# Eleven orders of the 512 columns in the products of a macaron feed-forward

## The chip, the cores and the metric

The kernel runs on one core of a Trainium2 chip. The metric is the device time of one execution in microseconds (us). Before the change it is 1822.53 us, the median of two runs (1821.94 and 1823.11). The profiled execution took 1822.9 us; its span, from the first to the last instruction, is 1821.1 us.

## The reference

One decoder layer works on 256 tokens of width 2048, all in float32. What matters here is the two half-step feed-forwards, with 5632 hidden columns each:

```python
def swiglu_ffn(x, w_gate, w_up, w_down):
    return (jax.nn.silu(x @ w_gate) * (x @ w_up)) @ w_down

h = h + 0.5 * swiglu_ffn(rms_norm(h, ffn1_norm[l]), ffn1_w_gate[l], ffn1_w_up[l], ffn1_w_down[l])
...   # one input projection, windowed attention and a state-space branch, one output projection
h = h + 0.5 * swiglu_ffn(rms_norm(h, ffn2_norm[l]), ffn2_w_gate[l], ffn2_w_up[l], ffn2_w_down[l])
```

## The kernel before

**Products.** Every large product is a list of passes (class `Pass`). A pass makes 512 output columns for all 256 tokens, so it needs two accumulators of 128 rows by 512 columns, one PSUM bank each. The activations, transposed, are the stationary operand (128 by 128), and the weights are the moving operand (128 by 512). For more than one rounding's accuracy both are split into a high and a low part in a rounded float32 type. Each block of 128 weight rows then takes three matmuls for each half of the tokens: high by high, high by low, low by high.

**The passes of a feed-forward** are made in `ffn`: for each of 11 blocks of hidden columns (c from 0 to 10) a pass of gate and a pass of up, 16 row blocks each; then four passes of down (n from 0 to 3), 44 row blocks each. The layer runs the first feed-forward, then the mixer's passes, then the second feed-forward.

**One loop for all of them.** `run` walks through the passes in units of two row blocks. For each unit it issues the matmuls of line 363, which is where all these products show in the profile. The order of work is written out by hand: a weight tile of four row blocks (`raw`, three buffers) is loaded on SP's queue, ScalarE copies it into the rounded type (`wh`, line 318), VectorE subtracts to get the low part (`wl`, line 323), four buffers of each, two row blocks long. The side work (norms, attention, scan) is cut into steps that are taken between units.

**What reads the accumulators.** After the last matmul of a pass its `done` function reads both accumulators whole: SiLU on ScalarE for gate (line 394), a product on VectorE for up (line 405), the residual sum for down (lines 438 and 447).

**Where the operands lie.** The normalised activations are `xth` and `xtl` (high and low), the hidden ones lie in several tiles named `hid` in the profile. `gap` tiles of 8 floats stand between some of them, so that tiles start at other places modulo 64 bytes.

**Other matmuls**, on lines of their own, belong to the mixer and to transposes. Line 733 streams 128 adjacent columns of one tile; line 796 streams four runs of 32 columns, 512 elements apart; both load 32 stationary columns. Line 831 loads its 32 stationary columns 64 elements apart, and line 834 loads them adjacent. Line 525 transposes with stationary columns 16 elements apart.

Of the kernel before, what the change touches and what calls it, by code (L numbers as in the profile page):

```python
# [16 lines left out]
P = 128  # L17
# [18 lines left out]
WB = 4  # L36


class Pass:
    def __init__(self, w, n, stat, ks, done=None, delay=0, pre=None, box=None, opens=True, bank="acc", shared=False):  # L40
        self.w, self.n, self.stat, self.ks, self.done = w, n, stat, list(ks), done
        self.delay, self.pre, self.opens, self.bank = delay, pre, opens, bank
        self.box = {} if box is None else box
        self.shared = shared
# [3 lines left out]
def hybrid_layer_kernel(  # L48
# [8 lines left out]
    act, vec, pe, pool, sync = nc.scalar, nc.vector, nc.tensor, nc.gpsimd, nc.sync  # L57
# [13 lines left out]
    def nm(s):  # L71
        uid[0] += 1
        return f"{s}_{uid[0]}"
# [9 lines left out]
    def tps():  # L83
        return tpp.tile([P, 512], F32, name=nm("tp"), tag="tp")
# [53 lines left out]
    def split_plain(h, l, src):  # L138
        act.activation(out=h, in_=src, func=AF.Copy)  # L139
        vec.tensor_tensor(out=l, in0=src, in1=h.bitcast(F32), op=ALU.subtract)  # L140
# [3 lines left out]
    def by_blocks(src, dst, pause=3):  # L144
        turns[0] += 1
        b = const.tile([P, 4, NT, P], F32, name=nm("blocks"), tag="blocks")
        hd = h_d[turns[0] % 2]
        for t in range(NT):
            vec.transpose(out=b[:, :, t].rearrange("p j (k c) -> p j k c", k=4),  # L149
                          in_=src[:, t, :].rearrange("p (k j c) -> p j k c", k=4, j=4))  # L150
        yield
        sync.dma_start(out=hd.rearrange("j p x -> p j x"), in_=b.rearrange("p j t x -> p j (t x)"))
        yield 2
        for j in range(4):
            sync.dma_start(out=dst[32 * j:32 * j + 32].rearrange("r (i x) -> r i x", i=4),
                           in_=hd[j].rearrange("(i r) x -> r i x", i=4))
        yield pause
        return dst.rearrange("p (i t x) -> p i t x", i=4, t=NT)
# [79 lines left out]
    def spawn(g, delay=0):  # L238
        gens.append([g, delay])
        return g  # L240
# [7 lines left out]
    def step():  # L248
        for e in list(gens):
            if e[1] > 0:  # L250
                e[1] -= 1
            else:
                advance(e)

    def call(f, a):
        f(a)
        return
        yield

    def alive(g):  # L260
        return any(e[0] is g for e in gens)

    def finish(*gs):
        while any(alive(g) for g in gs):
            step()

    def run(passes, extra, start):
        groups = []
        passes = list(passes)
        while passes:  # L270
            p = passes.pop(0)
            if p.shared:
                q = passes.pop(0)
# [55 lines left out]
        def ahead(u):  # L329
            while st["dma"] < ng and st["dma"] < spent() + RAWB:  # L330
                dma()
            if st["split"] == 0:
                start()
            while st["split"] < 2 * ng and st["split"] <= (u + WB - 1 if u else 1):
                split()
                if st["split"] == 1:
                    start()
                while st["dma"] < ng and st["dma"] < spent() + RAWB:
                    dma()

        for u, (i, half) in enumerate(units):
            p, k0 = groups[i]
            if k0 == p.ks[0] and half == 0:
                if p.pre:
                    p.pre()
                if p.opens:
                    p.box["acc"] = [tps() if p.bank == "tp" else
                                    accp.tile([P, 512], F32, name=nm("acc"), tag="acc") for _ in range(NT)]
            acc = p.box["acc"]
            ahead(u)  # L350
            h, l = wts.pop(u)
            end = half == 1 and k0 == p.ks[-1]
            order = [(kk, t, v) for kk in range(2) for t in range(NT) for v in range(3)]
            if u == 0:
                order = [(kk, t, v) for v in (0, 2, 1) for kk in range(2) for t in range(NT)]
            elif end:
                order = [(kk, t, v) for t in range(NT) for kk in range(2) for v in range(3)]
            for kk, t, v in order:
                k = k0 + 2 * half + kk
                sh, sl = p.stat(k)  # L360
                first = p.opens and k == p.ks[0] and v == 0
                last = p.done is not None and k == p.ks[-1] + 3 and v == 2
                pe.matmul(acc[t], (sh, sh, sl)[v][:, t * P:(t + 1) * P], (h, l, h)[v][:, kk, :], start=first, stop=last)  # L363
            if end and p.done:
                spawn(call(p.done, acc), p.delay)
            step()


    def ffn(norm, w_gate, w_up, w_down, done, first):
        hid = {}  # L370
        sil = {}
        pairs = {}
        area = {}
        turn = {}

        def hidden(c):
            tag = HID[c]
            if tag in ("slot0", "slot3"):
                if tag not in pairs:
                    pairs[tag] = slots.tile([P, 2, 2, 4, SEQ], F32R, name=nm("hid"), tag=tag)  # L380
                    return pairs[tag][:, 0]
                return pairs[tag][:, 1]
            return slots.tile([P, 2, 4, SEQ], F32R, name=nm("hid"), tag=tag)

        def gate_done(c):
            def f(acc):
                def g():
                    while c >= 2 and alive(turn[c - 2]):
                        yield
                    if c == 0:  # L390
                        area["a"] = slots.tile([P, 2, NT, 512], F32, name=nm("sil"), tag="s5b")
                    sil[c] = area["a"][:, c % 2]
                    for t in range(NT):
                        act.activation(out=sil[c][:, t, :], in_=acc[t], func=AF.Silu, scale=norm.scale(t))  # L394
                for _ in g() if c < 2 or not alive(turn[c - 2]) else ():
                    pass
                if c not in sil:
                    spawn(g())
            return f

        def up_done(c):
            def f(acc):
                a = sil.pop(c)
                for t in range(NT):
                    vec.scalar_tensor_tensor(out=a[:, t, :], in0=acc[t], scalar=norm.scale(t),  # L405
                                             in1=a[:, t, :], op0=ALU.mult, op1=ALU.mult)

                def g():
                    yield
                    while (c >= 5 and first and alive(mx["pre"])) or (c and alive(turn[c - 1])):  # L410
                        yield
                    hid[c] = hidden(c)
                    turned = yield from by_blocks(a, a.rearrange("p t x -> p (t x)"), 6)
                    for t in range(NT):
                        h, l = (hid[c][:, v, :, t * P:t * P + P].rearrange("p k (i c) -> p k i c", c=32) for v in range(2))
                        split_plain(h, l, turned[:, :, t].rearrange("p i (k c) -> p k i c", k=4))

                turn[c] = spawn(g())
            return f

        def hstat(k):
            c, kk = divmod(k, 4)
            return hid[c][:, 0, kk, :], hid[c][:, 1, kk, :]

        ps = []
        for c in range(DFF // 512):
            ps.append(Pass(w_gate, c, norm.stat, range(0, KD, 4), gate_done(c), 2,
                           (lambda: finish(mx["pre"])) if c == 7 and first else None, shared=c == 0))
            ps.append(Pass(w_up, c, norm.stat, range(0, KD, 4), up_done(c), 2))
        for n in range(4):  # L430
            ps.append(Pass(w_down, n, hstat, range(0, DFF // P, 4), done(n), 2 if n < 3 else 0))
        return ps

    def residual(norm, factor):
# [687 lines left out]
    with tc.manual_schedule():  # L1122
# [14 lines left out]
        ps = tps()  # L1137
# [52 lines left out]
        def start():  # L1190
# [6 lines left out]
            mx["go"] = True  # L1197

        ff1 = ffn(n1, ffn1_w_gate[0], ffn1_w_up[0], ffn1_w_down[0], residual(nmix, 0.5), True)
        mixp = mixer(nmix, residual(n2, 1.0))  # L1200
        ff2 = ffn(n2, ffn2_w_gate[0], ffn2_w_up[0], ffn2_w_down[0], lambda n: final(n), False)

        def load_x(n):
# [8 lines left out]
        def extra(n):  # L1212
            load_x(n)
            if 0 <= n - at - 6 < 4:
                load_m1(n - at - 6)

        run(ff1 + mixp + ff2, extra, start)


# [52 lines left out]
```

## Time and profile before

| What | Value |
|---|---|
| median of the runs | 1822.53 us |
| profiled execution | 1822.9 us |
| its span | 1821.1 us |
| TensorE busy, instructions | 1814.7 us, 8383 |
| weight loads busy | 1470.7 us |
| VectorE busy | 1061.5 us |
| ScalarE busy | 845.3 us |
| DMA | 404.31 MB, mean 222 GB/s |

A busy time is the union of an engine's instructions, so overlapping matmuls count once. In the groups of instructions each line has the source line, engine, operation, output and inputs, shapes and count; then the busy time, the mean duration of one instruction in ns, and the idle time of the engine before them. Matmuls are pipelined: one starts before the last has ended, and the distance from start to start is read from counts in windows or from starts in the timeline. The chain of waits follows back from the last instruction to what released it.

### The profile page before, as it was taken

How to read it: one execution, taken by the hardware profiler on the slowest of the kernel's cores; microseconds unless marked ns; L12 is line 12 of the kernel's file. 1: busy time of each engine (PE TensorE's matmuls, PEld its weight loads, DVE VectorE, ACT ScalarE, POOL GpSimd, SP SyncE). 2: the span in 40 equal slices, each digit the busy share in tenths (PEclk: the TensorE clock that was granted, in tenths of full speed). 3: DMA queues.
4: the chain of work that ended last, by engine and by line, in shares of the span. 5: the costliest groups of instructions: out<-in, count | busy, mean ns of one | idle time of the engine just before them, and what ended most of it. 6: DMA issues, size and time to landing. Idle time of an engine off the chain costs nothing.

```text
span 1821.1 us, 21499 instructions
## 1 busy us (share of the span) xinstructions
PE 1814.7 (100%) x8383; PEld 1470.7 (81%) x8383; DVE 1061.5 (58%) x1380; ACT 845.3 (46%) x1087; POOL 80.3 (4%) x151
## 2 busy tenths in 40 slices
PE   9999999999999999999999999999999999999999
PEld 7788888888888888888888888888888888888887
DVE  5779897555555455554975665555555555544443
ACT  6454444444444444447766554444444444443332
POOL 0301222000000000010000001000000000000000
PEclk9999999999999999999999999999999999999999
DMA  7867888786665566698475576666666666665553
GB/s 273 239 222 238 288 277 282 227 235 209 212 221 204 195 213 223 216 327 262 161 263 197 203 249 201 217 215 209 208 208 211 211 216 214 216 203 209 205 196 104
DMA packets 213237, 404.31 MB, mean 222 GB/s; under 512 B 9756, under 2 KB 43125, under 8 KB 211472
## 3 DMA queue, kind: packets, MB, share of 16 engines
q1 hardware_dynamic: 204896, 380.66, 64.5%
q0 software_dynamic: 6416, 19.13, 3.5%
q10 hardware_dynamic: 1824, 3.15, 0.7%
q8 instruction: 65, 1.06, 0.2%
q14 instruction: 36, 0.29, 0.0%
HBM read 371.05 MB, written 34.48 MB: 223 GB/s over the span
## 4 chain that ended last, share of the span: by engine, by line
PE 96%; DVE 2%; ACT 1%; DMA 1%; issue 0%; SPq 0%; ACTq 0%
PE acc L363 92%; PE tp L363 1%; DMA raw<-in_ffn_w_gate_dram 1%; DVE wl L323 1%; DVE s1a L820 0%; ACT wh L318 0%; PE tp L831 0%; DVE s1a L821 0%; PE tp L796 0%; PE tp L733 0%; ACT tp L895 0%; PE tp L1006 0%; PE tp L834 0%; DVE slot L822 0%; PE tp L905 0%
## 5 line engine op out<-in xcount | busy, mean ns | idle before, releaser
L323 DVE TENSOR_TENSOR wl<-raw,wh 128x1024 fp32r<-128x1024 f32 x628 | 768.3, 1225 | 712.4 <-ACT wh L318 712.2
L318 ACT ACTIVATE wh<-raw 128x1024 fp32r<-128x1024 f32 (+1 forms) x636 | 672.1, 1058 | 909.0 <-PE acc L363 879.9
L363 PE MATMUL acc<-wh,xth 128*128 128x512 f32 x1664 | 661.5, 398 | 0.0
L363 PE MATMUL acc<-wl,xth 128*128 128x512 f32 x1664 | 659.3, 396 | 0.0
L363 PE MATMUL acc<-wh,xtl 128*128 128x512 f32 x1664 | 652.0, 392 | 0.2 <-DVE xtl L188 0.2
L363 PE MATMUL acc<-wh,hid 128*128 128x512 f32 x1408 | 437.7, 392 | 0.0
L363 PEld LDWEIGHTS acc<-wh,xth 128*128 128x128 f32 x1664 | 312.0, 188 | 77.6 <-issue 1.6
L363 PEld LDWEIGHTS acc<-wh,xtl 128*128 128x128 f32 x1664 | 312.5, 188 | 74.7 <-DVE xtl L188 0.6
L363 PEld LDWEIGHTS acc<-wl,xth 128*128 128x128 f32 x1664 | 312.9, 188 | 69.2 <-DVE wl L323 0.2
L363 PEld LDWEIGHTS acc<-wh,hid 128*128 128x128 f32 x1408 | 264.4, 188 | 58.9
L363 PE MATMUL acc<-wl,hid 128*128 128x512 f32 x704 | 276.2, 392 | 0.0
L363 PEld LDWEIGHTS acc<-wl,hid 128*128 128x128 f32 x704 | 132.3, 188 | 29.5
L133 POOL TENSOR_TENSOR rs_t<-rstds 128x2 f32<-128x2 f32 x9 | 3.6, 396 | 670.6 <-DVE rstds L125 670.1
L449 POOL DMA_DIRECT2D out_dram<-res x6 | 3.3, 550 | 648.6 <-DVE res L447 648.5
L405 DVE SCALAR_TENSOR_TENSOR sil<-acc,rstds,sil 128x512 f32<-128x512 f32 x44 | 30.8, 741 | 0.0
L149 DVE STREAM_TRANSPOSE blocks<-sil 128x512 f32<-128x512 f32 x44 | 28.5, 686 | 0.0
L140 DVE TENSOR_TENSOR hid<-sil,hid 128x512 fp32r<-128x512 f32 x44 | 28.3, 683 | 0.0
L394 ACT ACTIVATE sil<-acc,rstds 128x512 f32<-128x512 f32 x44 | 27.5, 677 | 0.0
L139 ACT ACTIVATE hid<-sil 128x512 fp32r<-128x512 f32 x44 | 25.0, 615 | 0.0
L363 PE MATMUL acc<-wh,s2a 128*128 128x512 f32 x64 | 21.1, 397 | 0.0
L363 PE MATMUL acc<-wh,s4b 128*128 128x512 f32 x64 | 20.9, 396 | 0.0
L363 PE MATMUL acc<-wh,slot 128*128 128x512 f32 x64 | 20.8, 394 | 0.0
(310 smaller groups left out, 780.0 us busy)
## 6 DMA issues: line engine op xcount, KB each, us to landing
raw<-in_ffn_w_down_dram SPq DMA_DIRECT2D x88, 1024.0 KB, 5.1
raw<-in_ffn_w_gate_dram SPq DMA_DIRECT2D x87, 1024.0 KB, 5.8
raw<-in_ffn_w_up_dram SPq DMA_DIRECT2D x87, 1024.0 KB, 5.9
raw<-in_w_in_dram SPq DMA_DIRECT2D x32, 1024.0 KB, 5.6
raw<-in_w_out_dram SPq DMA_DIRECT2D x16, 1024.0 KB, 5.1
h_d<-blocks SPq DMA_DIRECT2D x30, 512.0 KB, 6.9
sil<-h_d SPq DMA_DIRECT2D x88, 128.0 KB, 7.2
m_d<-s4b POOLq DMA_DIRECT2D x16, 256.0 KB, 5.5
```

Of the source, the lines that this page charges most:

```text
L133: eng.tensor_tensor(out=tt, in0=out_t, in1=out_t, op=ALU.mult)
L139: act.activation(out=h, in_=src, func=AF.Copy)
L140: vec.tensor_tensor(out=l, in0=src, in1=h.bitcast(F32), op=ALU.subtract)
L149: vec.transpose(out=b[:, :, t].rearrange("p j (k c) -> p j k c", k=4), in_=src[:, t, :].rearrange("p (k j c) -> p j k c", k=4, j=4))
L318: act.activation(out=h[:, c], in_=src[:, c], func=AF.Copy)
L323: vec.tensor_tensor(out=l, in0=src, in1=h.bitcast(F32), op=ALU.subtract)
L363: pe.matmul(acc[t], (sh, sh, sl)[v][:, t * P:(t + 1) * P], (h, l, h)[v][:, kk, :], start=first, stop=last)
L394: act.activation(out=sil[c][:, t, :], in_=acc[t], func=AF.Silu, scale=norm.scale(t))
L405: vec.scalar_tensor_tensor(out=a[:, t, :], in0=acc[t], scalar=norm.scale(t), in1=a[:, t, :], op0=ALU.mult, op1=ALU.mult)
L449: (sync if n == 3 else pool).dma_start(out=out[0, t * P:(t + 1) * P, n * 512:(n + 1) * 512], in_=res[n][:, t, :])
```

## The change

The passes of the feed-forwards get an order, a `walk`, for their 512 columns. It is an access pattern that is laid over both the moving operand and the accumulator, so every column still meets its own place. `_mix(q, r)` cuts the columns into q equal parts and takes r adjacent columns of each part in turn, until all are done. `_back(r)` takes blocks of r columns from the last to the first, each block in its own order. Passes that set nothing keep the columns' plain order (the mixer's, gate and up of block 0, down pass 0).

| Passes | Order |
|---|---|
| gate and up, c = 1, 2, 3, 4 | quarters in turn by 2, 8, 16, 32 |
| c = 5, 6 | halves in turn by 16, 64 |
| c = 7, 8 | blocks of 16, of 64 from the end |
| c = 9, 10 | eighths in turn by 16; halves in turn by 4 |
| down, n = 1, 2, 3 | quarters by 16; blocks of 16 from the end; halves by 16 |

```diff
+def _mix(q, r):
+    return lambda x: x.rearrange("p (q a r) -> p a q r", q=q, r=r)
+
+
+def _back(r):
+    return lambda x: x.rearrange("p (a r) -> p a r", r=r)[:, ::-1]
+
+
+WALKS = (lambda x: x, _mix(4, 2), _mix(4, 8), _mix(4, 16), _mix(4, 32), _mix(2, 16), _mix(2, 64), _back(16), _back(64),
+         _mix(8, 16), _mix(2, 4))
+
+
 class Pass:
+    walk = staticmethod(WALKS[0])
+
...
-                pe.matmul(acc[t], (sh, sh, sl)[v][:, t * P:(t + 1) * P], (h, l, h)[v][:, kk, :], start=first, stop=last)
+                pe.matmul(p.walk(acc[t]), (sh, sh, sl)[v][:, t * P:(t + 1) * P], p.walk((h, l, h)[v][:, kk, :]),
+                          start=first, stop=last)
...
             ps.append(Pass(w_up, c, norm.stat, range(0, KD, 4), up_done(c), 2))
+            ps[-1].walk = ps[-2].walk = WALKS[c]
         for n in range(4):
             ps.append(Pass(w_down, n, hstat, range(0, DFF // P, 4), done(n), 2 if n < 3 else 0))
+            ps[-1].walk = WALKS[(0, 3, 7, 5)[n]]
```

## The prediction

> **What bounds the kernel now.** I read the page's head first, then the chain that ended last, then the groups, then windows of the span.
>
> ```profile
> span 1821.1 us, 21499 instructions
> PE 1814.7 (100%) x8383; PEld 1470.7 (81%) x8383; DVE 1061.5 (58%) x1380; ACT 845.3 (46%) x1087; POOL 80.3 (4%) x151
> PEclk9999999999999999999999999999999999999999
> PE 96%; DVE 2%; ACT 1%; DMA 1%; issue 0%; SPq 0%; ACTq 0%
> 306.21 513.23 PE acc L363 x2220
> 1022.12 794.52 PE acc L363 x3432
> ```
>
> TensorE is busy from end to end, its clock is granted at nine tenths or more in every slice, and the chain of waits is TensorE for 96%. In the last two rows, pieces of the chain in order of time, it runs the products of line 363 with no wait between them. So the kernel's time is a count of matmuls times the distance from one start to the next: 794.52 us over 3432 is 231.5 ns, 513.23 over 2220 is 231.2. The duration in the groups is another number:
>
> ```profile
> L363 PE MATMUL acc<-wh,xth 128*128 128x512 f32 x1664 | 661.5, 398 | 0.0
> L363 PE MATMUL acc<-wh,hid 128*128 128x512 f32 x1408 | 437.7, 392 | 0.0
> L363 PE MATMUL acc<-wl,hid 128*128 128x512 f32 x704 | 276.2, 392 | 0.0
> L363 PEld LDWEIGHTS acc<-wh,xth 128*128 128x128 f32 x1664 | 312.0, 188 | 77.6 <-issue 1.6
> 1400.00:1500.00 100.00, 100.00 (x432) 80.79 (x431) 4.21 (x6) 2.50 (x4) 1.00 0.67 210
> 1700.00:1800.00 100.00, 100.00 (x438) 81.85 (x437) 2.56 (x4) 0.00 (x0) 1.00 0.57 198
> ```
>
> One matmul lasts 392 to 398 ns, but they are pipelined, so the distance is what counts. The last two rows are windows of the second feed-forward, for the accumulator tiles alone: first figure the stretch, then TensorE's busy time and its matmuls. In the gate and up products 432 start in 100 us (231.5 ns), in the down products 438 (228.3 ns). The two differ in nothing but which tiles are read. So where the operands lie moves the distance by 3.2 ns. Loading the stationary operand takes 188 ns, which fits under each matmul.
>
> **The change, part by part.** No instruction is added, removed or moved and no wait changes: the same matmuls in the same order read the moving operand and write the accumulator column by column in another sequence. DMA queues, the splitting on ScalarE and VectorE and the reads of the accumulators are untouched, and each of those reads waits for a whole tile as before. The one thing that can change is the distance between starts, and nothing covers it: each nanosecond on each walked matmul is on the path.
>
> How many are walked: a pass of gate or up has 16 blocks of 128 rows, two row tiles and three products: 96 matmuls. A block c thus has 2 x 96 in each of two feed-forwards, 384. Blocks 1 to 10 are walked: 3840 matmuls. (Check: 22 passes x 96 x 2 plus 8 passes of the mixer x 96 is 4992, three groups of 1664.) A down pass has 44 x 2 x 3 = 264 (four passes make 1056 per feed-forward, 2112 in both: the rows' 1408 + 704). Its passes 1 to 3 are walked: 1584. Together 5424 of 7584.
>
> What one walked matmul costs more depends on how short its runs are. Block 1 has runs of 2 elements (256 jumps in a matmul), block 10 runs of 4 (128), block 2 runs of 8 (64). Blocks 3, 5, 7, 9 and the three down passes have runs of 16 (32 jumps), block 4 of 32 (16), blocks 6 and 8 of 64 (8).
>
> Line 363 shows no jump today; other products and ScalarE do.
>
> ```profile
> 176.03 1.01 PE tp L733 x32
> 830.28 1.01 PE tp L796 x32
> 64.88 1.03 PE tp L525 x8
> 929.93 0.53 PE L831 MATMUL tp<-s2a,slot 128*32 128x128 f32 x8
> 931.64 0.41 PE L834 MATMUL tp<-s2b,s1b 128*32 128x128 f32 x8
> ```
>
> The first three rows are from the chain, the others from the timeline (start, duration; x8 instructions). Line 733 streams 128 adjacent columns, line 796 streams 128 in four runs of 32 that lie 512 elements apart, and 32 instructions take 1.01 us in both. That is the same read that the change makes, with fewer jumps, at no price that shows.
>
> For short runs the nearest rows are stationary loads that fetch one element per jump. Line 525 loads 128 columns 16 elements apart: 1.03 us over 8 is 129 ns, 1.0 ns per jump. Line 831, alternating in eights with line 834's adjacent loads, loads 32 columns 64 elements apart: from 929.93 to 931.64 there are 56 instructions, 30.5 ns each, 0.95 ns per jump. A matmul of block 1 must make 256 jumps: 0.95 x 256 = 243 ns, 11.7 over today's 231.5, times 384 matmuls is 4.5 us; at 1.0 ns it is 256 ns, 9.4 us. In block 10 the same price gives 128 jumps in 122 ns, well under 231.5, so nothing, and the longer runs less still.
>
> ScalarE gives the far end:
>
> ```profile
> L527 ACT ACTIVATE s4a<-tp 128x512 f32<-128x512 f32 x2 | 2.1, 1054 | 0.7 <-PE tp L525 0.7
> L790 ACT ACTIVATE s1b<-tp 128x512 f32<-128x512 f32 x4 | 2.4, 590 | 0.0
> L839 ACT ACTIVATE s1a<-tp 128x512 f32<-128x512 f32 x4 | 2.3, 582 | 0.1
> L779 ACT ACTIVATE slot<-s1a 128x512 f32<-128x512 f32 x2 | 1.2, 624 | 3.1 <-DMA s1a<-u_d 3.1
> L1079 ACT ACTIVATE s1a<-s1a 128x512 f32<-128x512 f32 x4 | 2.5, 632 | 2.5 <-DVE s1a L1077 2.5
> ```
>
> All five move 512 columns. Line 527 writes each element 16 elements from the one before and takes 1054 ns where the adjacent write of line 790 takes 590: 0.91 ns more per jump. Line 839 writes in runs of 16 and takes 582, no more than adjacent; line 779 reads runs of 16, the rows from last to first, in 624 against 632 for adjacent reads (line 1079). So runs of 16 and blocks from the end are free on that engine, and single elements are not. At 0.91 ns per jump with nothing hidden, block 1 would cost 256 x 0.91 = 233 ns x 384 = 89 us, block 10 45 us and block 2 22 us.
>
> I take line 831's 4.5 us for block 1 and zero for all others: it is TensorE's own read, at the step nearest to the walk's (128 elements). The writing into the accumulators in runs is in no row at all, on any engine that writes as TensorE does; zero is my choice there, and the rivals hold its price.
>
> Last, where the operands' reads fall against each other is shuffled by a walk. The two windows bound that: gate and up could fall to 228.3 (3840 x 3.2 = 12 us less) or rise as much. I take zero.
>
> The sum, on the profiled execution: 1822.9 + 4.5 = 1827.4 us, of which 1.8 lie outside the 1821.1 span. The median of the runs shown, 1822.53, is 0.4 lower, which changes nothing. The case's own range is 1811 (12 less, and no 4.5) to 1845 (9.4 and 12 more).
>
> **The rivals.** *Short runs alone are slow (slower).* The moving read or the write of block 1, two elements at a time, cannot keep the pace, and each jump costs what line 527 shows: 89 us, 1912. For it: block 1 needs a jump every 231.5 / 256 = 0.90 ns, just under the 0.95 and 1.0 that loads show, and these loads do not have a write behind them. Against it: those rows are an upper bound on what the port can do, since each holds its instruction's own overhead too. It decides from 37 us, 95 ns on each of the 384.
>
> *Every run pays at the accumulator (slower).* The accumulators add to what is there; if each jump breaks that by one column, every order is hit. One column is 228.3 / 512 = 0.45 ns. The jumps are 384 x (256 + 128 + 64) for blocks 1, 10 and 2, 32 x (4 x 384 + 1584) for runs of 16, 384 x 16 for block 4 and 768 x 8 for 6 and 8: 172,032 + 99,840 + 6,144 + 6,144 = 284,160. That makes 127 us, 1950; at line 527's 0.91 ns it would be 2081. It decides from 37 us / 284,160 = 0.13 ns per jump. For it: no row shows a broken write by TensorE. Against it: ScalarE's runs of 16 at 582 ns. [...]
>
> *The places fall badly, or well.* Single distances spread more widely than the means:
>
> ```profile
> 1500.29 0.40 PE L363 MATMUL acc<-wl,xth 128*128 128x512 f32 x1
> 1500.53 0.39 PE L363 MATMUL acc<-wh,xtl 128*128 128x512 f32 x1
> ...
> 1502.86 0.39 PE L363 MATMUL acc<-wh,xth 128*128 128x512 f32 x1
> 1503.08 0.39 PE L363 MATMUL acc<-wl,xth 128*128 128x512 f32 x1
> ```
>
> They run from 0.22 to 0.24 us. With every walked matmul at 0.24, gate and up lose 8.5 ns x 3840 and down 11.7 x 1584: 51 us, 1874. At 0.22 they gain 11.5 x 3840 + 8.3 x 1584 = 57 us, 1766. Eleven orders that all fall to one side are unlikely.
>
> *It does not do what it says.* Blocks 0 and down pass 0 keep their order, the rest are walked on both operands alike; I see no way for it to be without effect on the order, so this gets no chance of its own.
>
> **How the numbers follow.** Forecast 66%, short runs alone 12%, every run 13%, bad places 4%, good places 5%. About 2%, 36 us, is what a measurement of this kernel can tell from no change, so the bounds are 1786 and 1859. Forecast lies within; short runs, every run and bad places are slower: 29%; good places faster: 5%. The range takes in the forecast's own 1811 to 1845, bad places and short runs up to 1915; it leaves out every run and good places, 18%.
>
> **What would show it.** The instruction count stays 21499. In windows of the second feed-forward, block 1 (about 1128 to 1172 us) should have 400 to 411 accumulator matmuls per 100 us in place of 432 (243 to 250 ns), and block 10 (about 1529 to 1574) 432. If short runs alone are slow, block 1 shows about 215 (464 ns) and takes 89 us more over both feed-forwards, while blocks with runs of 16 keep 432. If every run pays, runs of 16 show 246 ns (406 per 100 us), in the down passes too. The forecast is wrong if any order with runs of 8 or more leaves the band of 0.22 to 0.24 us.

## The result and the profile after

The changed kernel takes 1929.35 us (median of two runs, 1929.21 and 1929.48), against 1822.53 before: 1.059 times as long, with a 95% interval of 1.054 to 1.063. The forecast was 1827 with a range up to 1915, so the time lies 14 us above the range, on the slower side.

The head of the page after, with the groups of the largest products:

```profile
span 1927.7 us, 21495 instructions
PE 1921.3 (100%) x8383; PEld 1482.9 (77%) x8383; DVE 1062.2 (55%) x1380; ACT 846.0 (44%) x1087; POOL 81.1 (4%) x151
PEclk9999999999999999999999999999999999999999
PE 96%; DVE 2%; ACT 1%; DMA 1%; issue 0%; SPq 0%; ACTq 0%
L377 PE MATMUL acc<-wh,xth 128*128 128x512 f32 x1664 | 696.3, 419 | 0.0
L377 PE MATMUL acc<-wh,hid 128*128 128x512 f32 x1408 | 444.4, 397 | 0.0
```

TensorE runs the same 8383 matmuls with the same clock and is busy all the time, as before; VectorE's and ScalarE's work has not changed by a microsecond. (Of all instructions there are 21495 in place of 21499, but the counts of the five engines on the second line are the same.) The chain of waits is TensorE for the same 96%. So the loss is in the distance from one start to the next, and the two long pieces of the chain hold 63.5 us of it (start and length in us):

```profile
349.20 523.54 PE acc L377 x2220
1075.48 847.71 PE acc L377 x3432
```

The second was 794.52 before with the same 3432 matmuls: 53 us more, the loss of one feed-forward. In the first feed-forward the walked blocks 1 to 5 lie ahead of the other piece, which therefore starts 43 us later than before (349.20 against 306.21) and is itself only 10 us longer. Windows of the second feed-forward show which blocks pay. Each window is one block of gate and up, 192 matmuls (the counts include one or two that reach over an edge); first the stretch, then TensorE's time with its matmuls. In order: block 0 (plain), 1 (quarters by 2), 3 (quarters by 16), 5 (halves by 16), 9 (eighths by 16), 10 (halves by 4):

```profile
1136.40:1181.10 44.70, 44.70 (x194) 36.08 (x193) 0.95 (x2) 1.27 (x2) 1.00 0.68 207
1181.10:1266.40 85.30, 85.30 (x194) 39.54 (x193) 1.40 (x2) 1.25 (x2) 1.00 0.39 121
...
1311.20:1355.80 44.60, 44.60 (x194) 36.03 (x193) 1.40 (x2) 1.25 (x2) 1.00 0.72 212
...
1401.00:1447.10 46.10, 46.10 (x194) 36.59 (x193) 1.40 (x2) 1.25 (x2) 1.00 0.70 207
...
1581.40:1627.10 45.70, 45.70 (x194) 36.33 (x193) 1.41 (x2) 1.25 (x2) 1.00 0.66 209
1627.10:1675.60 48.50, 48.50 (x193) 36.34 (x192) 1.40 (x2) 1.28 (x2) 1.00 0.62 198
```

Block 1 takes 85.3 us where a plain block takes 44.7: 444 ns per matmul, 40.6 us more, 81 in both feed-forwards. Block 10 takes 3.8 us more, block 5 1.4, block 9 1.0. From the starts in the trace, the distance in ns by order (median and mean; in plain order 232 and 232.4 for gate and up, 228 and 229.6 for down):

```
quarters by 2    445  445.8     quarters by 8   232  234.2     halves by 4     253  252.8
halves by 16     240  240.3     eighths by 16   238  237.7     quarters by 16  233  232.7
quarters by 32   235  235.8     halves by 64    232  232.7     16 from the end 235  234.9
64 from the end  232  232.4
down: quarters by 16  233 232.7    16 from the end  234 234.7    halves by 16  240 240.0
```

Block 1 carries 81 of the 107 us. Block 10 gives 8, and the orders by 16 (three blocks of gate and up and the three down passes) most of the rest.

### The profile page after: what moved, and what is told of

It reads as the page before. It is cut to its first block, busy times and chain, and to the rows that moved or that the text cites. A ratio compares the mean times of both kernels' runs of the same rounds, so it can differ in the third digit from the quotient of the medians.

```text
span 1927.7 us, 21495 instructions
## 1 busy us (share of the span) xinstructions
PE 1921.3 (100%) x8383; PEld 1482.9 (77%) x8383; DVE 1062.2 (55%) x1380; ACT 846.0 (44%) x1087; POOL 81.1 (4%) x151
## 4 chain that ended last, share of the span: by engine, by line
PE 96%; DVE 2%; ACT 1%; DMA 1%; issue 0%; SPq 0%; ACTq 0%
PE acc L377 93%; PE tp L377 1%; DMA raw<-in_ffn_w_gate_dram 1%; DVE wl L337 1%; DVE s1a L837 0%; ACT wh L332 0%; PE tp L848 0%; DVE s1a L838 0%; PE tp L750 0%; PE tp L813 0%; ACT tp L912 0%; PE tp L1023 0%; PE tp L851 0%; DVE slot L839 0%; PE tp L922 0%
## 5 line engine op out<-in xcount | busy, mean ns | idle before, releaser
L377 PE MATMUL acc<-wh,xth 128*128 128x512 f32 x1664 | 696.3, 419 | 0.0
L377 PE MATMUL acc<-wl,xth 128*128 128x512 f32 x1664 | 691.5, 416 | 0.0
L377 PE MATMUL acc<-wh,xtl 128*128 128x512 f32 x1664 | 689.8, 415 | 0.2 <-DVE xtl L202 0.2
L377 PE MATMUL acc<-wh,hid 128*128 128x512 f32 x1408 | 444.4, 397 | 0.0
```

What stands on the lines that cost most here:

```text
L377: pe.matmul(p.walk(acc[t]), (sh, sh, sl)[v][:, t * P:(t + 1) * P], p.walk((h, l, h)[v][:, kk, :]), start=first, stop=last)
```

## Experiments

Two questions were open: whether the read of the moving operand or the write into the accumulators is slow, and why. Ratios with an interval come from four or five executions of a kernel; the other kernels were executed once. For the orders, "quarters by 2" stands for two columns of each quarter in turn, and so on.

**Read or write.** The line that issues the products, with the walk on one side alone:

```diff
-                pe.matmul(p.walk(acc[t]), (sh, sh, sl)[v][:, t * P:(t + 1) * P], p.walk((h, l, h)[v][:, kk, :]),
+                pe.matmul(acc[t], (sh, sh, sl)[v][:, t * P:(t + 1) * P], p.walk((h, l, h)[v][:, kk, :]),   # read only
+                pe.matmul(p.walk(acc[t]), (sh, sh, sl)[v][:, t * P:(t + 1) * P], (h, l, h)[v][:, kk, :],   # write only
```

> The eleven orders are laid over the moving operand alone; the accumulators are written in the plain order, so the output columns of the feed-forwards come out permuted. In the changed kernel block 1 (quarters by 2) stands at 445 ns from start to start and block 10 (halves by 4) at 253, plain blocks at 232. Theory A, the read of the moving operand is what is slow: 445 and 253 again, about 1929 us. Theory B, the write into the accumulator is slow: all blocks at 232, about 1823 us. Theory C, both take part: block 1 between, near 340 ns.

> The eleven orders are laid over the accumulators alone; the moving operand is read in the plain order, so output columns are permuted. Theory A (read): all blocks at 232 ns, about 1823 us. Theory B (write): block 1 at 445 ns, block 10 at 253, about 1929 us. Theory C: block 1 near 340 ns.

Read only took 1929.94 us, write only 1823.04, beside 1823.33 for the kernel before. Windows of blocks 1, 5 and 10 of the second feed-forward, read only:

```profile
1181.50:1266.80 85.30, 85.30 (x193) 39.57 (x192) 1.41 (x2) 1.25 (x2) 1.00 0.37 121
1401.40:1447.50 46.10, 46.10 (x193) 36.57 (x192) 1.41 (x2) 1.25 (x2) 1.00 0.68 208
1627.50:1676.10 48.60, 48.60 (x194) 36.40 (x193) 1.41 (x2) 1.28 (x2) 1.00 0.61 197
```

The same blocks, write only:

```profile
1127.80:1172.50 44.70, 44.70 (x194) 36.10 (x193) 1.40 (x2) 1.25 (x2) 1.00 0.70 220
1306.30:1351.00 44.70, 44.70 (x194) 36.09 (x193) 1.40 (x2) 1.25 (x2) 1.00 0.69 214
1529.50:1574.10 44.60, 44.60 (x194) 36.02 (x193) 1.40 (x2) 1.25 (x2) 1.00 0.65 211
```

Theory A holds without a remainder: the read carries the whole loss, to a tenth of a microsecond in the three blocks shown, and the write costs nothing in any of the eleven orders.

**Is the loss that of block 1?** One kernel put block 1 back to the plain order, the other walked block 1 alone:

```diff
-            ps[-1].walk = ps[-2].walk = WALKS[c]
+            ps[-1].walk = ps[-2].walk = WALKS[c if c != 1 else 0]     # block 1 plain
+            ps[-1].walk = ps[-2].walk = WALKS[c if c == 1 else 0]     # block 1 alone; down passes plain
```

> The changed kernel with block 1 of gate and up put back to the plain order, the other walks kept. If the runs of 2 alone carry the loss, 384 x (445 - 232) ns = 82 us go: 1929 - 82 = 1847 us, ratio 1.014. If every jump pays alike, 107 us over 284,160 jumps is 0.38 ns each and block 1's 98,304 jumps give back 37 us: 1892 us, ratio 1.038.

> Only block 1 of gate and up is walked (quarters by 2), everything else plain. If the runs of 2 alone carry the loss: 1822.5 + 82 = 1904 us, ratio 1.045. If every jump pays alike: 1822.5 + 37 = 1860 us, ratio 1.020. If the walks add up without meeting, this run's gain over the kernel before and the one with block 1 plain sum to the whole 107 us.

Block 1 plain: 1847.97 us, ratio 1.0135 (1.0118 to 1.0152). Block 1 alone: 1905.14 us, ratio 1.0449 (1.0433 to 1.0464). Both lie about 1 us from the theory of the short runs and 44 and 45 us from that of equal jumps. The two losses over the kernel before, 24.6 and 81.8 us, sum to 106.4, the whole.

**Which short runs, and why.** The next kernel read in ten other orders (`_mix` and `_back` with other numbers, read side only):

> Ten other orders, over the moving operand alone (output columns permuted), down passes plain. Blocks 1 to 10: halves by 2, eighths by 2, first pairs of every four then second pairs, blocks of 2 from the end, blocks of 4 from the end, single columns from the end, evens then odds, quarters by 4, eighths by 4, quarters by single columns. Theory F, a fetch brings four adjacent columns (16 bytes) and takes four columns' time, about 1.67 ns, and what is not used in a row is lost: blocks 1, 2, 3 and 7 make 256 fetches and stand at 445 ns; block 4, whose pairs sit in one four, at 232 if the fetch is kept and at 445 if not; block 5 at 232; block 6 at 232 if the fetch is kept; blocks 8 and 9 at 232 to 253; block 10 makes 512 fetches: 512 x 1.67 + 18 = 871 ns. Theory J, each jump to another place costs 0.83 ns, whatever is fetched: blocks 1 to 4 at 445, block 5 at 338, blocks 6, 7 and 10 at 658. Total by F with kept fetches: 1823 + 0.384 x (4 x 213 + 639) = 2396 us.

The distances in ns, by the starts in the trace (median, mean):

```
halves by 2         329  332.6     blocks of 2 from the end      233  233.9
eighths by 2        487  489.5     blocks of 4 from the end      233  233.8
first pairs of every four, then
second pairs        453  453.1     single columns from the end   233  233.8
evens, then odds    453  454.3     quarters by single columns    275  277.9
quarters by 4       268  267.9     eighths by 4                  278  277.9
```

Windows of blocks 1 (halves by 2), 2 (eighths by 2), 6 (single columns from the end) and 10 (quarters by single columns):

```profile
1305.70:1369.50 63.80, 63.80 (x193) 37.45 (x192) 1.40 (x2) 1.25 (x2) 1.00 0.50 162
1369.50:1463.20 93.70, 93.70 (x193) 40.08 (x192) 1.41 (x2) 1.26 (x2) 1.00 0.32 101
...
1639.80:1684.60 44.80, 44.80 (x193) 36.09 (x192) 1.41 (x2) 1.25 (x2) 1.00 0.68 210
...
1876.70:1930.00 53.30, 53.30 (x193) 36.44 (x192) 1.40 (x2) 1.25 (x2) 1.00 0.56 177
```

The whole run took 2179.01 us, not F's 2396. Theory J falls at once: single columns from the end make 511 jumps and cost 1 ns (233.8 on average, against 232.7 in the same block before). Theory F comes within 10 ns on five orders: the two of pairs and singles at 453 and the three from the end. Eighths by 2 (487 against 445) and the two by 4 (268 and 278 against 232 to 253) lie above it, and it is far too dear on two: halves by 2 (329, not 445) and quarters by single columns (275, not 871). A piece that was left seems to be kept, in some orders.

> Ten orders over the moving operand alone (output columns permuted), down passes plain. Blocks 1 to 10: halves, eighths and sixteenths by single columns, sixteenths, thirty-seconds and sixty-fourths by 2, every fourth column, every eighth column, thirty-seconds by 8, sixteenths by 8. Theory G: four columns that follow each other are served together, and each distinct 16-byte four of the row among them that is not still held takes a step of 227 / 128 = 1.77 ns. Then halves by 1 stand where halves by 2 stood (329 ns), the three orders by 2 at 445 to 490, every fourth and every eighth column at four steps per group, 907 ns, and eighths and sixteenths by 1 at 907 as well if no more than four are held, or near 280 if more are. Theory K: jumping between far places is cheap and pairs are what is dear: all single columns near 275 as quarters by 1 were, all orders by 2 at 445 to 490. By both, by 8 about 232 to 245.

Blocks 1, 2 and 7 (halves by single columns, eighths by single columns, every fourth column):

```profile
1420.50:1462.00 41.50, 41.50 (x194) 36.32 (x193) 1.40 (x2) 1.25 (x2) 1.00 0.75 233
1462.00:1556.10 94.10, 94.10 (x194) 40.13 (x193) 1.41 (x2) 1.25 (x2) 1.00 0.34 107
...
1898.20:1986.70 88.50, 88.50 (x193) 39.90 (x192) 1.40 (x2) 1.25 (x2) 1.00 0.34 107
```

The run took 2407.42 us. Halves by single columns stand at 216 ns, *faster than plain* (41.5 us for 192 matmuls against 44.7), every fourth column at 461, every eighth at 431, eighths by single columns at 487, sixteenths by single columns at 434; orders by 2 between 432 and 461; thirty-seconds and sixteenths by 8 at 231. So theory G falls (nothing goes to 907, and halves by single columns are nowhere near 329), and K too (eighths and sixteenths by single columns are dear).

What fits is a third theory, S: two columns are served at a time, by two streams, the odd and the even places of the order, and each stream keeps the 16-byte piece of the row (four columns) that it last read. In halves by single columns each stream has its own half and needs a new piece every four of its columns, 64 in a matmul: 216 ns. In plain order, and backwards, both streams step through the same pieces and each needs a new one every second of its columns, 128: 227 to 239, by where the tiles lie (below). Where every column of a stream lies in another piece (every fourth column; evens, then odds; quarters, eighths and others by 2), it needs 256: 431 to 490. It was made from those runs, so it was tested on new orders: column j with column j + D, in turn.

```diff
+def _cross(b, a):
+    return lambda x: x.rearrange("p (q b a) -> p q a b", b=b, a=a)
+WALKS = (lambda x: x, _cross(2, 4), _cross(2, 8), _cross(2, 16), _cross(2, 32), _cross(2, 64), _cross(2, 128), _cross(2, 2), _cross(4, 4),
+         _cross(4, 32), _cross(8, 4))
```

> Ten orders over the moving operand alone (output columns permuted), down passes plain. Blocks 1 to 6: column j and column j + D in turn, in neighbouring blocks of D, for D = 4, 8, 16, 32, 64, 128; block 7 the same with D = 2; blocks 8 and 9: four columns D = 4 and D = 32 apart in turn; block 10: eight columns 4 apart in turn. Theory S: two streams, odd and even in the order, each keeping its 16-byte piece: D = 4 to 128 all near 216 ns, D = 2 near 232, blocks 8 and 9 near 275 like quarters by single columns, block 10 near 487 like eighths by single columns. Theory G, four columns served together: D = 4 to 128 near 329 like halves by 2. Theory B, the distance decides: 216 only at the largest distances, short ones at 232 or above.

Block 1 (D = 4), 6 (D = 128), 7 (D = 2), 8 (four columns, 4 apart), 10 (eight columns, 4 apart):

```profile
1172.60:1214.10 41.50, 41.50 (x194) 36.30 (x193) 1.40 (x2) 1.25 (x2) 1.00 0.78 232
...
1379.80:1421.30 41.50, 41.50 (x194) 36.32 (x194) 1.40 (x2) 1.25 (x2) 1.00 0.74 228
1421.30:1465.90 44.60, 44.60 (x193) 36.03 (x192) 1.40 (x2) 1.25 (x2) 1.00 0.70 216
1465.90:1517.50 51.60, 51.60 (x193) 36.34 (x192) 1.40 (x2) 1.25 (x2) 1.00 0.59 190
...
1569.80:1661.90 92.10, 92.10 (x193) 40.33 (x192) 1.41 (x2) 1.25 (x2) 1.00 0.32 104
```

The run took 1910.87 us. All six distances from 4 to 128 stand at 216 ns, D = 2 at 232, the four columns at 269 and 273, the eight at 480. S gave the first seven from its count of pieces; G (329) and B (only the largest distance) fail. What S does not derive are the orders in which a stream goes to and fro between two pieces: 269 to 275 for single columns, 329 for halves by 2. For four and eight columns the expectations went by likeness, and how far a stream can keep a second piece stays open. Nor did any order tell two streams with a piece each from one pair of pieces that both share; halves by single columns with every second pair turned round would have, and was not run. S is thus the simplest account that fits, not a mechanism that was seen.

**The small extras.** Halves by 4 stand 20 ns over plain though each stream takes two columns of a piece, as in plain order; halves by 16 stand 8 over.

> Ten orders with whole fours, over both operands. Blocks 1 to 10: eighths by 8, sixteenths by 4, thirty-seconds by 4, halves by 8, halves by 32, eighths by 4, quarters by 4, quarters by 64, halves by 128, sixty-fourths by 4; down passes plain. Theory D, the small extra (253 ns for halves by 4, 240 for halves by 16, 232 for quarters by 8 or 16) hangs on the distance of the jump: halves (1024 bytes) cost, so halves by 8 at 245 or so, halves by 32 at 236, and quarters by 4 at 232. Theory N, it hangs on the number of jumps: all orders by 4 at 253 and all by 8 or more at 232 to 236. Total: 1825 by D; by N 5 blocks x 384 x 21 ns more, 1863 us.

Windows of sixteenths by 4 and thirty-seconds by 4:

```profile
1197.10:1244.20 47.10, 47.10 (x193) 36.63 (x192) 1.40 (x2) 1.25 (x2) 1.00 0.63 198
1244.20:1287.60 43.40, 43.40 (x194) 36.00 (x193) 1.40 (x2) 1.25 (x2) 1.00 0.71 216
```

Median and mean in ns: by 4, halves 253 (the changed kernel's), quarters 267 (267.7), eighths 278 (278.0), sixteenths 246 (246.7), thirty-seconds 225 (225.9), sixty-fourths 232 (232.0). By 8, halves 243 (243.4), eighths 245 (246.7); halves by 32 236 (236.6); quarters by 64 and halves by 128 232 (232.4). The run took 1867.15 us. N fails, since sixteenths by 4 and thirty-seconds by 4 make the same 128 jumps and differ by 21 ns, and so does D, since quarters by 4 cost more than halves. With the number of jumps alike, the extra changes with the distance of the jump, but not in proportion to it.

The other suspect was the load of the next stationary operand, which runs under each matmul (188 ns, and in the trace of before it starts with the matmul that it runs under). In the trace of before, plain orders, the mean distance in ns by the place of the next stationary operand against the moving one, modulo 256 bytes (places from the kernel's own allocation):

```
 0: 228.5    32: 238.1    64: 231.6    96: 232.4   128: 232.3   160: 235.1   192: 230.3   224: 232.9
```

Two kernels put all tiles of the large products at one place modulo 256, one in plain order, one with the change's eleven orders:

```diff
-            const.tile([P, 8], F32, name=nm("gap"), tag=f"gap{v}{tag}")
+    const.tile([P, 40], F32, name=nm("gap"), tag="gap")
...
-        if tag in order[:5]:
-            slots.tile([P, 8], F32, name=nm("gap"), tag=f"gap{tag}")
```

> The kernel before, plain orders, with the small gap tiles taken out and one of 160 bytes put in, so that all moving and all stationary tiles of the large products start at the same place modulo 256 bytes. Theory P, the distance between starts hangs on where the next stationary operand lies against the moving one: in the trace of before, pairs at the same place modulo 256 stand at 228.5 ns on average and pairs 32 bytes on at 238; then all stand near 228.5 and the time falls by some 7584 x 2.5 ns = 19 us, to about 1804. If place plays no part: 1823 us.

> The changed kernel with the same placing of tiles, all at one place modulo 256 bytes. Theory P2, the small extras of halves by 16 (240), eighths by 16 (238) and halves by 4 (253) come from meeting the load of the next stationary operand in one place: they move with the placing, by several ns. Theory Q, the moving read hinders itself: 240, 238 and 253 stay. Runs of 2 stay at 445 by both.

The plain one took 1789.38 us, ratio 0.9814 (0.9801 to 0.9828): 34 us less, more than the 19 expected. Two windows of it, in gate and up and in down:

```profile
1100.00:1200.00 100.00, 100.00 (x443) 82.84 (x442) 2.80 (x4) 3.76 (x6) 1.00 0.69 212
1600.00:1700.00 100.00, 100.00 (x443) 82.84 (x442) 2.56 (x4) 0.00 (x0) 1.00 0.59 200
```

It was 432 in gate and up before; now both stages stand at 227 ns by the starts, so where operands lie is worth 2% of this kernel. The place modulo 256 is not the whole rule: pairs at place 0 stood at 228.5 in the kernel before, with its mixed places, and stand at 226.7 here. With the eleven orders it took 1913.34 us, 124 more than the plain one. Its blocks 5 (halves by 16) and 10 (halves by 4):

```profile
1389.00:1435.10 46.10, 46.10 (x193) 36.48 (x193) 1.41 (x2) 1.25 (x2) 1.00 0.67 207
...
1613.00:1661.00 48.00, 48.00 (x194) 36.29 (x193) 1.41 (x2) 1.28 (x2) 1.00 0.62 200
```

Plain blocks fell to 227, but halves by 16 stayed at 240, eighths by 16 at 239, halves by 4 at 250, quarters by 2 at 445 (means): as far as this one placing can show, Q holds for the extras, and they belong to the moving read itself. By which rule of distance stays open.

**What beats both kernels.** Thirty-seconds by 4 was the one order of the change's kind well below plain. It was laid over all large products, once with all tiles at one place modulo 256, once with every stationary tile 192 bytes on.

> The kernel before with all tiles at one place modulo 256 bytes (as in the aligned run, 1789 us) and every large product, the mixer's too, walked in thirty-seconds by 4, the one order that stood below plain (225.9 against 232.4 ns). Theory P3: that order meets the stationary load less; with places alike it stood at 225.9 on average, so little is gained on 227: 1785 to 1790 us. Theory R: its gain over plain (6.5 ns) adds to that of the placing (4 ns): 7584 x 6.5 = 49 us less, 1740.

> As the run before it, but with every stationary tile 192 bytes behind the moving ones modulo 256, the place where thirty-sevenths did not, and thirty-seconds by 4 did, show the least: 222 ns on average, 220 in the middle. Theory P3: 7584 x 5 ns less than the aligned plain order: about 1752 us. If place does nothing for this order: as the run before it.

(In the last text the words on "thirty-sevenths" are a slip and say nothing.) They took 1787.10 us, ratio 0.9803 (0.9788 to 0.9817), and 1755.45 us, ratio 0.9626 (0.9610 to 0.9643). P3 had 1785 to 1790 and 1752; R had 1740 for the first and fails. So this order's distance does depend on where the stationary tiles lie, by 32 us. The plain order was not run at that place, so how much of this is the order's own stays open.

The last kernel used S with the tiles where they were before. It reads halves by single columns and writes the accumulator plainly; what reads the accumulators takes every second column and so restores the order:

```diff
-                pe.matmul(acc[t], (sh, sh, sl)[v][:, t * P:(t + 1) * P], (h, l, h)[v][:, kk, :], start=first, stop=last)
+                pe.matmul(acc[t], (sh, sh, sl)[v][:, t * P:(t + 1) * P], (h, l, h)[v][:, kk, :].rearrange("p (q a) -> p a q", q=2),
+                          start=first, stop=last)
...
-                spawn(call(p.done, acc), p.delay)
+                spawn(call(p.done, [x.rearrange("p (a q) -> p q a", q=2) for x in acc]), p.delay)
...
-                        act.activation(out=sil[c][:, t, :], in_=acc[t], func=AF.Silu, scale=norm.scale(t))
+                        act.activation(out=halves(sil[c][:, t, :]), in_=acc[t], func=AF.Silu, scale=norm.scale(t))
```

(`halves` views 512 columns as two rows of 256, and the other readers are changed likewise.)

> The kernel before, with its own placing of tiles, where every large product reads its moving operand in single columns from the two halves in turn and writes the accumulator in plain order; what reads the accumulators puts the columns back by reading every second one. Theory S (and every theory that takes the 216 ns of halves by single columns as it is): 7584 matmuls go from 231 to 216 ns, 114 us less, if ScalarE and VectorE lose nothing on reading every second column and the splitting keeps up with twelve matmuls in 2.6 us: 1709 us, ratio 0.938. If the splitting or the strided reads become the bound: between 1709 and 1823.

It took 1711.77 us, ratio 0.9390 (0.9377 to 0.9402). From its page and groups, then windows of block 1 (192 matmuls) and of a down pass (264):

```profile
span 1709.3 us, 21495 instructions
PE 1697.4 (99%) x8383; PEld 1480.3 (87%) x8383; DVE 1059.4 (62%) x1380; ACT 839.5 (49%) x1087; POOL 82.4 (5%) x151
L410 DVE SCALAR_TENSOR_TENSOR sil<-acc,rstds,sil 128x512 f32<-128x512 f32 x44 | 30.8, 742 | 0.0
L399 ACT ACTIVATE sil<-acc,rstds 128x512 f32<-128x512 f32 x44 | 27.6, 681 | 1.4 <-POOL rstds L140 1.3
```

```profile
1062.30:1103.70 41.40, 41.40 (x193) 36.26 (x192) 1.40 (x2) 1.25 (x2) 1.00 0.77 235
1533.70:1590.60 56.90, 56.90 (x265) 49.84 (x264) 1.28 (x2) 0.00 (x0) 1.00 0.62 211
```

Both stand at 216 ns. Reading every second column of an accumulator costs VectorE 1 ns and ScalarE 4 over the 741 and 677 of before. The splitting keeps up nearly everywhere: TensorE is idle for 12 us of the span, where it was for 6. This is 111 us below the kernel before and 218 below the changed one.

## Why the prediction was wrong

**What held.** The kernel is bound by the distance between starts, nothing covers it, no other engine plays a part, and the count of walked matmuls is right: 384 x 213 ns is the 82 us that block 1 alone costs. The zero chosen for the write into the accumulators, the term with no row, was right as well, but by luck: no row spoke for it.

**The step that failed** is the price of block 1. It was taken from line 831, "0.95 x 256 = 243 ns", 4.5 us in all, and measured 445 ns and 82 us. That row is a stationary load. I took it for the same read because it is TensorE's, but the moving read of quarters by 2 pays 445 / 256 = 1.74 ns per run of two (by theory S, a new piece for each of two streams at every run), where the load pays 0.95 per column. Nor was 0.95 a price of jumps. It averages the loads of line 831 with the adjacent ones of line 834, and these follow each other almost as slowly:

```profile
930.25 0.42 PE L834 MATMUL tp<-s2b,s1b 128*32 128x128 f32 x8
930.47 0.44 PE L831 MATMUL tp<-s2a,slot 128*32 128x128 f32 x8
930.72 0.41 PE L834 MATMUL tp<-s2b,s1b 128*32 128x128 f32 x8
930.93 0.44 PE L831 MATMUL tp<-s2a,slot 128*32 128x128 f32 x8
```

Eight of line 834 take 0.21 to 0.22 us from start to start, eight of line 831 take 0.25: at most a few ns of a load of 32 columns can be the price of its jumps. The row of line 796, with its moving read in runs of 32, could not have shown the price either: in the change runs of 32 cost about 3 ns.

**The rival that came true** is the short runs alone, given 12%. Its place was right, and its 89 us, by ScalarE's line 527, was near the 82 measured. That the two lie so near is luck: the rival added 0.91 ns per jump to the plain distance, while 256 runs of two at 1.74 ns are the whole 445. It also had blocks with runs of 16 unchanged, and they were not. Set against it I had written that the load rows are an upper bound on what the port can do. That the load and the moving read share one is in no run, and the moving read took 1.74 ns per run of two against the loads' 0.95 and 1.0 per jump.

**What pushed it out of the range** are the other 25 us. Runs of 4, priced at nothing because 128 jumps fit under 231.5 ns, cost 20 ns a matmul (8 us). Runs of 16, free on ScalarE by line 779 and line 839, cost 8 to 10 in halves and 5 in eighths. What was free on another engine was not free here. The sum left them at zero, and the range added only bad places to the forecast, not bad places to the rival.

**The rival of every run** (13%) is refuted by the two kernels that split read and write. *Places*: the two stages do differ, by 2.8 ns by the starts (232.4 and 229.6; the windows that gave 3.2 count matmuls that reach over an edge), and place is worth more than that, since placing tiles gave 34 us. But the changed kernel's loss is not in it: halves by 64 and 64 from the end, walked too, stand at the plain 232.

**Two neighbours in a row do not settle it.** Quarters by 2 have just two in a row and take 445 ns, 1.9 times the plain 232, while halves by single columns never have two in a row and take 216; no order took less. By theory S it is each of the two streams that needs its own neighbours.

## What to carry to other kernels

Where TensorE is bound by its moving operand in 4-byte elements, try reading it so that odd and even places of the order walk through different pieces of the row (columns j and j + D in turn, D a power of two from 4 to 256 in these runs): 216 ns in place of 232 for 512 columns, and the readers of the accumulator undid the order for at most 4 ns a tile. Do not read it in runs of 2 that jump to another part of the row (329 to 490 ns). A price taken from another engine, or from the other operand of the same engine, was a bound in neither direction here: runs of 16 were free on ScalarE and cost 8 to 10 ns in halves, runs of 2 in quarters took 1.74 ns each against the load's 0.95 per column, and 511 jumps of single columns from the end cost 1 ns.

## What the runs showed of the hardware

- The accumulators can be written in any of the eleven orders at no cost (1823.04 us against 1823.33). Writes in single columns were not run.
- Counted by theory S, an account and not a mechanism that was seen, the moving read of 512 columns in this type takes 216 ns where each stream needs 64 new four-column pieces, 227 to 239 in plain order with 128, and 431 to 490 with 256. Two groups lie between: runs of 4 to 32 that jump (128 pieces too) took 225 to 278, and the orders that go to and fro between two pieces 269 to 329. No order took more than 490 on average, however scattered the columns.
- Plain order does not reach the best: it stands 11 to 22 ns above 216 (226.7 with all tiles at one place, 238.1 in the worst place of the kernel before). In that kernel the means ran from 228.5 to 238.1 by how the next stationary operand lies against the moving one modulo 256 bytes. In halves by single columns, at the kernel's own mixed places, gate and up (41.4 us for 192 matmuls) and down (56.9 us for 264) both stand at 216, where in plain order they lie 2.8 ns apart: nothing of that dependence is seen in the means.
- Backward reads cost little: single columns, blocks of 2, 4 and 64 about 1 ns or less, blocks of 16 2.5 ns in gate and up and 5 in down.
